# Moving ScalarE's roundings behind copies and squares, and the modulation steps to other places, in a two-layer decoder trunk

## The chip, the cores and the metric

The kernel runs on one core of a Trainium2 chip. The metric is the device time of one execution in microseconds (us). Three runs of the kernel before took 1254.53, 1255.86 and 1257.47 us, with a median of 1255.86 us. The profile shows one further execution.

## The reference

The reference is a decoder trunk of two layers over 512 tokens of 1024 channels, in float32. Layer 0 mixes tokens with a state-space model (S5), layer 1 with forgetting attention (FoX, 16 heads of 64). Behind each mixer stands a gated network with a causal convolution of width 3. Each of the four sub-layers is normalised, shifted, scaled and gated by numbers made from a conditioning vector `c` ("modulation").

```
def modulate(x, g, shift, scale):
    return rmsnorm(x, g) * (1.0 + scale) + shift
...
    mod = jax.nn.silu(c) @ w + b                      # per sub-layer: 3 x 1024 outputs
    shift, scale, gate = jnp.split(mod, 3, axis=-1)
...
    log_f = jax.nn.log_sigmoid((f_logit + b_f).astype(f32))     # fox
    F = lax.cumsum(log_f, axis=1).transpose(0, 2, 1)
    s = q k^T + F[..., None] - F[:, :, None, :]        # causal softmax, then @ v, then @ w_out
...
    up = h @ w_up                                     # network, D_FF = 2816
    a, b = jnp.split(up, 2, axis=-1)
    a_conv = causal width-3 convolution of a
    return (jax.nn.silu(a_conv) * b) @ w_down
```

## The kernel before, in words

All activations lie channel by token, in eight tiles of 128 channels by 512 tokens. Each float32 product is made from two rounded parts per operand: `put_parts` writes `hi`, the rounding of a tile, on ScalarE (ACT, line 256), and `lo`, the rest, on VectorE (DVE, line 257), and TensorE (PE) adds the products hi*hi, lo*hi and hi*lo (line 273). A weight tile comes from memory as `raw` and becomes `w_hi` and `w_lo`; there are five buffers of each of the latter two.

**The program's stages in time.** S5 and its products run to 285 us, with the first network's opening products from about 205 us on in between; the first network runs to 605 us, its last product, the norm, the attention's values and the forget logits to 690 us, the attention's heads to 860 us, the attention's output product and norm to 935 us, the second network to 1200 us, and its tail to 1252 us.

**The networks** (`ffn`) loop over 22 columns f of 128 gated channels. In most columns `quarters` makes both halves of the up-product with seven half-size products of 256 tokens (`times`, line 523) in place of eight, by a Strassen scheme. For that DVE makes four weight sums (`sums`, line 495) of the two `raw` tiles, and ACT and DVE round those as well. The products accumulate in PSUM tiles `p1`, `p5` (`mmp`) and `p2`, `p4` (`aux`). `p1` is used in steps: once a11*b11 is in it, ACT copies it to `nm_h` (line 530, `c1`), s2*t2 is added and it is copied again (`c2`), then s3*t3 is added. So PE can't add s3*t3 before ACT has made the copy `c2`. `gated` then makes the convolution (ACT line 570, two DVE steps at line 572), the activation (ACT line 575), the gating product (DVE line 579) and its rounding (`ghi`, `glo`). Columns 0, 1, 2, 3, 6, 11 and 17 of the first network are made plainly, without sums. Behind each column stand one or two tiles of the down-product (`down`) of the group of columns before.

**The modulation steps** (`ada_units`) are background work: a weight tile of 512 KB is brought by a DMA that GpSimd (POOL) issues at line 213 into a room (`ada_raw` in the first network), and one DVE instruction (line 226) multiplies and sums it. A call of `tick(n)` issues n such steps where it stands, and `behind(...)` orders a step behind the instructions in `self.evac`. In the first network a tick stands ahead of and behind each column's down-product, and `evac` names the last rounding `glo`. In the attention the rooms are the tiles `s3`, `phi` and `plo`, and later weight buffers that `w_hi` and `w_lo` share.

**The squares.** The norm's sum of squares is gathered while the last product still runs: after each residual step (DVE `h`, line 339) ACT squares the tile (`nm_t`, line 331), DVE adds it to `ssq` (line 333), and PE sums over the channels (`aux<-ones,ssq`, line 357). ACT also rounds the attention's first weights (`fox_vf`, `fox_v`) in this stretch.

**The forget logits.** The values' product (line 1317) also gives 16 logits a token. `log_forget` is a chain of 37 small DVE steps on 128x64 elements (`lf_ring`, up to `lf_out` at line 693). PE waits for it at line 1277 (the running sum).

A scheduler places each instruction in its engine's queue by readiness and the edges that the code adds; each engine then works its queue in order.

Of the kernel before, what the change touches and what calls it, by code (L numbers as in the profile page):

```python
# [17 lines left out]
P = 128  # L18
# [30 lines left out]
THIRDS = ((1, 2), (2, 0), (2, 1), (2, 2), (3, 0), (3, 1), (3, 2))  # L49
QK = 6  # L50
# [7 lines left out]
class Trunk:  # L58
# [6 lines left out]
    def __init__(self, tc, io, ctx):  # L65
# [14 lines left out]
        self.normed, self.evac = [], []  # L80
# [116 lines left out]
    def ada_units(self, *thirds, rooms=("ada_raw",), late=True):  # L197
# [3 lines left out]
        todo = [(i, t, j) for i, t in thirds for j in range(KT)]  # L201
# [17 lines left out]
        for n, (i, t, j) in enumerate(todo):  # L219
            if not late:  # L220
                load(n + ahead)
            if j == 0:
                sums = self.bgpool.tile([P, KT], F32, name="ada_s", bufs=2)
# [99 lines left out]
    def square(self, m, cols, eng=None):  # L323
# [7 lines left out]
        nc.scalar.activation(sq[:, cols], self.h[:, m, cols], AF.Square)  # L331
# [155 lines left out]
    def quarters(self, pool, l, f, x, finish):  # L487
# [8 lines left out]
        w = {}  # L496

        def parts(src, names, *where):
# [3 lines left out]
            self.put_parts(hi, lo, src)  # L502
# [25 lines left out]
        def copy(o):  # L528
            t = self.tmp.tile([P, N], F32, name="nm_h", bufs=4)
            nc.scalar.activation(t, o, AF.Copy)  # L530
            return t
# [11 lines left out]
        c2 = copy(p1)  # L543
# [10 lines left out]
    def ffn(self, i, l, x, nxt, ticks=0, plain=None):  # L554

        nc, tc = self.nc, self.tc
        with tc.tile_pool(name=f"ffn{l}", bufs=1, reuse_waits="tile") as pool:
# [8 lines left out]
            def gated(m, ps, cols):  # L566
                f = m // 2
                if m % 2 == 0:
                    t = pool.tile([P, S], F32, name="conv", bufs=2 if plain else 3)
                    nc.scalar.activation(t, ps, AF.Identity, bias=cb[:, f:f + 1], scale=cw[:, 2, f:f + 1])  # L570
                    for d in (1, 2):
                        nc.vector.scalar_tensor_tensor(
# [3 lines left out]
                    keep[f] = t  # L576
                    return
# [8 lines left out]
                self.evac = [self.put_parts(hi[:, j, :], lo[:, j, :], t).ins]  # L586
# [12 lines left out]
            for q, n in enumerate(groups):  # L599
# [6 lines left out]
                for j, f in enumerate(fs):  # L606
# [14 lines left out]
                    if q:  # L621
                        self.tick(ticks)
# [125 lines left out]
class S5(Trunk):  # L748
# [292 lines left out]
    def s5(self, i, nxt):  # L1041
# [186 lines left out]
        with tc.tile_pool(name="s5b", bufs=1, reuse_waits="tile") as pool:  # L1228
# [10 lines left out]
            self.bg = [self.ada_units((1, 2), rooms=("ada_raw", "ada_raw2"))]  # L1239
# [11 lines left out]
class Kernel(S5):  # L1251
# [32 lines left out]
    def fox_values(self, pool, x):  # L1284
# [9 lines left out]
        def load(q):  # L1294

            src = self.io["fox_v"][q - 1] if q else self.io["fox_vf"]
            n, step = (W, 4) if q else (W + NH, 3)
            out = []
            for a in range(0, KT, step):
                j = min(step, KT - a)  # L1300
                hi, lo = self.split(src[:, a:a + j, :], [P, j, n])
                out += [(hi[:, i, :], lo[:, i, :]) for i in range(j)]
            return out

        def values(qs, blocks, w, aux=()):
# [15 lines left out]
            for q, b in todo:  # L1321
# [3 lines left out]
                if b % 2:  # L1325
                    self.tick(1)
# [3 lines left out]
        w = {q: load(q) for q in range(2)}  # L1330
# [4 lines left out]
        for q in range(2, NV):  # L1335
            values((q,), range(NB), {q: load(q)})
        return lf

    def fox(self, i, x, nxt):
        with self.tc.tile_pool(name="fox", bufs=1, reuse_waits="tile") as pool:  # L1340
            self.bgpool = pool
            self.fox_heads(pool, x)
            after, y = nxt
            self.product(
                self.io["fox_w_out"], range(KT), KT, lambda k: (self.o[k][:, 0], self.o[k][:, 1]),
                self.add_residual(i), head=4, tail=2, after=after,
                halves=(slice(0, S),), step=self.unit, ticks=1,
# [3 lines left out]
    def fox_heads(self, pool, x):  # L1351
# [14 lines left out]
        def project(m, ps, cols):  # L1366
# [11 lines left out]
            self.evac = [part.ins]  # L1378
            if m % 2 == 0:
# [205 lines left out]
```

## Time and profile before

| | |
|---|---|
| median of 3 runs | 1255.86 us (1254.53 to 1257.47) |
| profiled execution | 1253.84 us, of which the span of the profile is 1252.0 us |
| PE busy | 1214.2 us, 97% |
| DVE busy | 1007.0 us, 80% |
| ACT busy | 612.4 us, 49% |
| GpSimd busy | 89.1 us, 7% |
| first network, 205 to 605 us | PE 392.02 us, DVE 342.11 us, ACT 186.31 us |
| second network, 935 to 1200 us | PE 265.00 us, DVE 224.63 us, ACT 142.15 us |

A row of the waits reads: engine and line that waited, the engine and line that ended the wait, the sum in us, how often, the longest. A row of the timeline reads: start, duration, engine, line, operation, what it writes and from what, with the idle time ahead of it in brackets. PEclk is the share of its full clock that the throttle granted TensorE.

### The profile page before, as it was taken

To read this page: it belongs to the slowest core of one execution; us is meant where nothing else is said; L and a number is where in the kernel's file an instruction comes from. 1 tells how busy PE (TensorE), PEld (TensorE's weight loads), DVE (VectorE), ACT (ScalarE), POOL (GpSimd) and SP (SyncE) were. 2 spreads that over 40 slices of the span, in tenths; PEclk is the share of its full clock that TensorE was granted. 3 is DMA by queue.
4 is the path that set the end of the run, shared out by engine and by line. 5 is a ranking of instruction groups with operands and counts; after the bars stand their busy time and mean duration, and the time that the engine had idled before them with its cause. 6 is when DMAs were issued, how large, how long until landed. Compare 5 with 4: busy or idle time off the path is not lost.

```text
span 1252.0 us, 20635 instructions
## 1 busy us (share of the span) xinstructions
PE 1214.2 (97%) x7921; PEld 1038.0 (83%) x7921; DVE 1007.0 (80%) x1871; ACT 612.4 (49%) x1137; POOL 89.1 (7%) x143
## 2 busy tenths in 40 slices
PE   7999999999999989999998999999999999999997
PEld 2566678898989889899798888877989999999987
DVE  7888986779889988888777577865799888888855
ACT  3544465335544444444533465663356545555543
POOL 0000000100000000000000344530000000000000
PEclk9999999999999989999999999999999999999999
DMA  9677778521354545443615544422213332332321
GB/s 366 227 231 241 220 226 280 194 80 43 126 183 137 184 153 173 147 160 131 213 52 188 170 145 147 166 82 68 87 51 110 118 120 83 106 119 89 102 85 68
DMA packets 74385, 183.83 MB, mean 147 GB/s; under 512 B 23231, under 2 KB 25631, under 8 KB 73263
## 3 DMA queue, kind: packets, MB, share of 16 engines
q1 hardware_dynamic: 68239, 161.02, 38.5%
q0 software_dynamic: 5760, 20.97, 5.0%
q8 instruction: 62, 1.02, 0.3%
q10 hardware_dynamic: 288, 0.52, 0.1%
q14 instruction: 36, 0.29, 0.1%
HBM read 175.57 MB, written 6.92 MB: 146 GB/s over the span
## 4 chain that ended last, share of the span: by engine, by line
PE 66%; issue 19%; DVE 8%; DMA 4%; ACT 1%; POOL 1%; SPq 0%; DVEq 0%; POOLq 0%; ACTq 0%
PE mmp L273 28%; PE mmp L523 12%; PE aux L523 5%; PE mmp L1131 4%; DVE w_lo L257 2%; PE aux L937 2%; PE mmp L1317 2%; PE aux L1468 2%; PE mmp L1160 2%; PE aux L1026 1%; PE mmp L184 1%; PE aux L1018 1%; PE aux L1451 1%; PE aux L1421 1%; DMA raw<-in_w_up 1%
## 5 line engine op out<-in xcount | busy, mean ns | idle before, releaser
L256 ACT ACTIVATE w_hi<-raw 128x1024 fp32r<-128x1024 f32 (+4 forms) x205 | 176.7, 866 | 168.4 <-PE mmp L273 81.3
L257 DVE TENSOR_TENSOR w_lo<-raw,w_hi 128x1024 fp32r<-128x1024 f32 (+4 forms) x205 | 202.0, 992 | 30.3 <-ACT w_hi L256 30.0
L273 PE MATMUL mmp<-ghi,w_hi 128*128 128x512 f32 (+1 forms) x392 | 148.2, 378 | 0.0
L273 PE MATMUL mmp<-glo,w_hi 128*128 128x512 f32 (+1 forms) x392 | 147.6, 376 | 0.0
L273 PE MATMUL mmp<-ghi,w_lo 128*128 128x512 f32 (+1 forms) x392 | 147.3, 376 | 0.0
L273 PE MATMUL mmp<-a_hi,w_hi 128*128 128x512 f32 (+1 forms) x376 | 139.5, 374 | 1.5 <-ACT a_hi L410 1.5
L273 PE MATMUL mmp<-a_lo,w_hi 128*128 128x512 f32 (+1 forms) x376 | 137.2, 365 | 0.0
L273 PE MATMUL mmp<-a_hi,w_lo 128*128 128x512 f32 (+1 forms) x376 | 137.1, 365 | 0.0
L523 PE MATMUL mmp<-w_hi 128*128 128x256 f32 x396 | 111.8, 282 | 7.0 <-ACT nm_h L530 7.0
L523 PE MATMUL mmp<-w_lo,w_hi 128*128 128x256 f32 x396 | 110.9, 280 | 0.0
L523 PE MATMUL mmp<-w_hi,w_lo 128*128 128x256 f32 x396 | 110.7, 279 | 0.0
L256 ACT ACTIVATE w_hi<-sums 128x1024 fp32r<-128x1024 f32 x74 | 78.4, 1059 | 56.6 <-DVE sums L495 43.2
L257 DVE TENSOR_TENSOR w_lo<-sums,w_hi 128x1024 fp32r<-128x1024 f32 x74 | 90.3, 1220 | 5.0 <-ACT w_hi L256 4.5
L339 DVE SCALAR_TENSOR_TENSOR h<-mmp,par,h 128x512 f32<-128x512 f32 (+1 forms) x100 | 68.4, 684 | 25.8 <-PE mmp L273 25.5
L273 PEld LDWEIGHTS mmp<-ghi,w_lo 128*128 128x128 f32 x392 | 75.2, 192 | 14.4
L273 PEld LDWEIGHTS mmp<-ghi,w_hi 128*128 128x128 f32 x392 | 75.5, 193 | 13.0
L273 PEld LDWEIGHTS mmp<-glo,w_hi 128*128 128x128 f32 x392 | 75.3, 192 | 12.9
L273 PEld LDWEIGHTS mmp<-a_hi,w_hi 128*128 128x128 f32 x376 | 70.9, 190 | 14.4 <-issue 2.6
L523 PEld LDWEIGHTS mmp<-w_hi 128*128 128x128 f32 x396 | 75.6, 191 | 8.0 <-ACT nm_h L530 8.0
L273 PEld LDWEIGHTS mmp<-a_hi,w_lo 128*128 128x128 f32 x376 | 71.4, 190 | 12.0 <-DVE w_lo L257 0.6
L273 PEld LDWEIGHTS mmp<-a_lo,w_hi 128*128 128x128 f32 x376 | 71.4, 190 | 9.9
L523 PEld LDWEIGHTS mmp<-w_lo,w_hi 128*128 128x128 f32 x396 | 75.2, 190 | 0.0
(313 smaller groups left out, 3013.5 us busy)
## 6 DMA issues: line engine op xcount, KB each, us to landing
raw<-in_w_up SPq DMA_DIRECT2D x88, 512.0 KB, 3.3
raw<-in_ada_w SPq DMA_DIRECT2D x40, 512.0 KB, 6.4
ada_raw<-in_ada_t POOLq DMA_DIRECT2D x40, 512.0 KB, 3.9
raw<-in_w_down SPq DMA_DIRECT2D x32, 320.0 KB, 3.2
nf<-nfd SPq DMA_DIRECT2D x8, 1152.0 KB, 6.4
raw<-in_fox_qk SPq DMA_DIRECT2D x16, 512.0 KB, 4.4
raw<-in_w_down SPq DMA_DIRECT2D x24, 256.0 KB, 3.3
raw<-in_w_down SPq DMA_DIRECT2D x16, 384.0 KB, 3.1
```

Of the source, the lines that this page charges most:

```text
L184: self.last_mm = nc.tensor.matmul(ps[32 * qq:32 * qq + 32, :], self.sc32[:, k, :], w[:, q * S:(q + 1) * S], start=(step is steps[0]), stop ...
L256: nc.scalar.activation(hi, src, AF.Copy)
L257: return nc.vector.tensor_tensor(lo, src, hi.bitcast(F32), ALU.subtract)
L273: self.last_mm = self.nc.tensor.matmul(o, wt, xt[:, cols], start=(k == 0 and n == 0), stop=(k == nk - 1 and n == 2),)
L339: add = self.nc.vector.scalar_tensor_tensor(self.h[:, m, cols], ps, self.par[i][:, 16 + m:17 + m], self.h[:, m, cols], op0=ALU.mult, op1=A ...
L523: self.last_mm = nc.tensor.matmul(o, wt[:, k], xt[:, k], start=(first and k == 0 and n == 0), stop=(k == H - 1 and n == 2), skip_group_che ...
L937: nc.tensor.matmul(ps[g2][:, j, cols], x[rows, a + j, r].rearrange("p c j -> p (c j)"), self.rr[rows, planes, q, :], start=(j == 0 and r = ...
L1018: nc.tensor.matmul(yp[g2][:, k, :], t[:, g].rearrange("p c i -> p (c i)"), u[:, g, :], start=(k == 0), stop=False, skip_group_check=True,)
L1131: nc.tensor.matmul(ps, w[m][:, k, :], x[:, k], start=(k == 0), stop=(k == KT - 1))
L1160: nc.tensor.matmul(gps[m], wt, xt[:, k], start=(k == 0 and part == 0 and xt is yhi), stop=(k == KT - 1 and part == 1))
L1317: self.last_mm = nc.tensor.matmul(ps[q, b][:, :n], xt[:, k, tb], wt, start=(k == 0 and i == 0), stop=(k == KT - 1 and i == 2),)
L1468: nc.tensor.matmul(pv[:, c * P:], self.v[:, hp, k, r].rearrange("p t d -> p (t d)"), pp[:, r, c + 3 * k:NB + 3 * k, :].rearrange("p b t -> ...
```

## The change

No instruction is added or taken away: the change is one of order, with the rooms of some modulation steps.

- In `quarters`, the roundings of a column stand behind the copy `c2` of the column before (`self.copied`).
- In the first network, the first of a column's two ticks moves from behind the column to the end of the convolution's second DVE step, and the steps are ordered behind that step instead of behind `glo`.
- The roundings of the attention's first weights, but the first piece of each, stand behind the last square of the first half (`self.squared`), and the pieces of two quarters of heads alternate.
- Among the attention's values, ticks stand at five blocks of the first two quarters of heads (before: at every second block of all), so that steps stand ahead of the forget chain and not inside it.
- In the heads, the tick moves from the projections to behind the last rounding of a head pair's turned weights (`plo`).
- The last two steps are given the rooms `s3` and `nf` in place of weight buffers, and ticks at tiles 4 and 5 of the output product.

The diff, cut:

```diff
@@ squares
+            a = nc.scalar.activation(sq[:, cols], self.h[:, m, cols], AF.Square)
+        if m == KT - 1 and cols.start == 0:
+            self.squared = [a.ins]
@@ quarters
+        copied = self.copied
...
-            self.put_parts(hi, lo, src)
+            with self.behind(*copied):
+                self.put_parts(hi, lo, src)
...
-        def copy(o):
+        def copy(o, last=False):
             t = self.tmp.tile([P, N], F32, name="nm_h", bufs=4)
-            nc.scalar.activation(t, o, AF.Copy)
+            a = nc.scalar.activation(t, o, AF.Copy)
+            if last:
+                self.copied = [a.ins]
             return t
...
-        c2 = copy(p1)
+        c2 = copy(p1, True)
@@ gated, in ffn
-                        nc.vector.scalar_tensor_tensor(
+                        c = nc.vector.scalar_tensor_tensor(
                             t[:, d:], ps[:, :S - d], cw[:, 2 - d, f:f + 1], t[:, d:], op0=ALU.mult, op1=ALU.add
                         )
                     nc.scalar.activation(t, t, AF.Silu)
                     keep[f] = t
+                    if plain and f >= groups[0]:
+                        self.evac = [c.ins]
+                        self.tick(ticks)
                     return
...
-                self.evac = [self.put_parts(hi[:, j, :], lo[:, j, :], t).ins]
+                self.put_parts(hi[:, j, :], lo[:, j, :], t)
@@ ffn
                     if q:
-                        self.tick(ticks)
                         down(q - 1, range(j * KT // n, (j + 1) * KT // n))
                         self.tick(ticks)
@@ fox_values
+        def load(qs):
+
+            out = {q: [] for q in qs}
+            for c in range(3):
+                for q in qs:
...
+                    with self.behind(*(self.squared if 0 in qs and c else ())):
+                        hi, lo = self.split(src[:, a:a + j, :], [P, j, n])
...
-                if b % 2:
+                if todo[0][0] == 0 and (b != 1 or q):
                     self.tick(1)
@@ fox
+            def add(m, ps, cols):
+                residual(m, ps, cols)
+                if m in (4, 5):
+                    self.tick(1)
...
-                halves=(slice(0, S),), step=self.unit, ticks=1,
+                halves=(slice(0, S),), step=self.unit,
@@ fox_heads
-            self.evac = [part.ins]
-            if m % 2 == 0:
+            if m == 0:
                 self.tick(1)
@@ turn
+            if b == NB - 1:
+                self.evac = [part.ins]
+                self.tick(1)
@@ the whole
-        k.bg = [k.ada_units((3, 1), rooms=("s3", "phi", "plo"), late=False), k.ada_units((3, 0), rooms=(1, 2), late=False)]
+        k.bg = [
+            k.ada_units(units((3, 1))[:7], rooms=("s3", "phi", "plo"), late=False),
+            k.ada_units(units((3, 1))[7:] + units((3, 0))[:6], rooms=(1, 2), late=False),
+            k.ada_units(units((3, 0))[6:], rooms=("s3", "nf"), late=False),
+        ]
```

**What it moves, at three places.** The first is ACT's queue in column 12 of the first network, at about 444 us of the profile. The numbers behind the names are those of the buffers; `mmp_4305` is column 12's `p1`, while the `raw` and `sums` tiles are those of column 13. Before:

```order
L530 ACTIVATE nm_h_4323<-mmp_4305 128x256
L530 ACTIVATE nm_h_4337<-mmp_4306 128x256
L256 ACTIVATE w_hi_4470<-raw_4464 128x1024
L256 ACTIVATE w_hi_4476<-sums_4468 128x1024
L530 ACTIVATE nm_h_4364<-mmp_4305 128x256
L256 ACTIVATE w_hi_4486<-raw_4466 128x512
```

After the change:

```order
L536 ACTIVATE nm_h_4323<-mmp_4305 128x256
L536 ACTIVATE nm_h_4337<-mmp_4306 128x256
L536 ACTIVATE nm_h_4364<-mmp_4305 128x256
L258 ACTIVATE w_hi_4470<-raw_4464 128x1024
L258 ACTIVATE w_hi_4476<-sums_4468 128x1024
L258 ACTIVATE w_hi_4486<-raw_4466 128x512
```

The copy `c2` (the third `nm_h`) moved ahead of the two roundings.

The second is ACT's queue at the squares, at about 612 us; the `raw` tiles are the first weights of the attention's values. Before:

```order
L256 ACTIVATE w_hi_6396<-raw_6398 128x544
L331 ACTIVATE nm_t_6064<-h_1962 128x512
L256 ACTIVATE w_hi_6402<-raw_6404 128x1024
L331 ACTIVATE nm_t_6090<-h_1962 128x512
L256 ACTIVATE w_hi_6408<-raw_6410 128x1024
L331 ACTIVATE nm_t_6116<-h_1962 128x512
L331 ACTIVATE nm_t_6160<-h_1962 128x256
```

After the change:

```order
L333 ACTIVATE nm_t_6090<-h_1962 128x512
L333 ACTIVATE nm_t_6116<-h_1962 128x512
L333 ACTIVATE nm_t_6160<-h_1962 128x256
L333 ACTIVATE nm_t_6180<-h_1962 128x256
L333 ACTIVATE nm_t_6200<-h_1962 128x256
L333 ACTIVATE nm_t_6220<-h_1962 128x256
L258 ACTIVATE w_hi_6396<-raw_6398 128x816
L258 ACTIVATE w_hi_6402<-raw_6404 128x1024
L258 ACTIVATE w_hi_6408<-raw_6410 128x544
```

Three roundings moved behind seven squares (the first stands ahead of this piece, `nm_t_6064`).

The third is DVE's queue at the head of the output product, at about 861 us; `raw` under line 226 (228 after the change) is the room of a modulation step, and `w_lo_8814` (`w_lo_8809` after) the weight of output tile 4. Before:

```order
L339 SCALAR_TENSOR_TENSOR h_1962<-mmp_8538,par2_97,h_1962 128x512
L226 ISA raw_8434,ada_s_7175<-raw_8434,c_row_1970 128x1024
L226 ISA ada_s_7175 128x1
L339 SCALAR_TENSOR_TENSOR h_1962<-mmp_8539,par2_97,h_1962 128x512
L233 TENSOR_TENSOR par3_98<-ada_s_7175,rest_126 128x8
L339 SCALAR_TENSOR_TENSOR h_1962<-mmp_8540,par2_97,h_1962 128x512
L333 TENSOR_TENSOR ssq_8797<-ssq_8797,nm_t_8802 128x512
L339 SCALAR_TENSOR_TENSOR h_1962<-mmp_8541,par2_97,h_1962 128x512
L333 TENSOR_TENSOR ssq_8797<-ssq_8797,nm_t_8806 128x512
L257 TENSOR_TENSOR w_lo_8814<-raw_8815,w_hi_8813 128x1024
```

After the change, from a place some 32 rows earlier in the queue, while the last head pair still runs:

```order
L228 ISA raw_8284,ada_s_7445<-raw_8284,c_row_1970 128x1024
L228 ISA ada_s_7445 128x1
L259 TENSOR_TENSOR w_lo_8528<-raw_8529,w_hi_8527 128x1024
L259 TENSOR_TENSOR lo_8502<-mmp_8437,hi_8501 128x512
L259 TENSOR_TENSOR w_lo_8809<-raw_8810,w_hi_8808 128x1024
```

The rounding of tile 4's weight moved ahead of the last head pair's work; the last modulation steps now stand behind tile 4's and tile 5's residual steps (not shown).

More of the change, by code (lines that the diff above doesn't have):

```diff
@@ L195, in ada_pe, with ada_units @@
             yield True
-    def ada_units(self, *thirds, rooms=("ada_raw",), late=True):
+    def ada_units(self, todo, rooms=("ada_raw",), late=True):
         nc = self.nc
-        todo = [(i, t, j) for i, t in thirds for j in range(KT)]
         ws = {}
@@ L221, in ada_units @@
                 load(n + ahead)
[L222 to L223 removed]
+            if (i, t) not in self.sums:
+                self.sums[i, t] = self.bgpool.tile([P, KT], F32, name="ada_s", bufs=2)
+            sums = self.sums[i, t]
             w = ws.pop(n)
```

33 lines of the change are left out of this document (17 added, 16 removed).

## The prediction

> **What bounds the kernel now.** I read the page's first part, then the waits of TensorE (PE), then the stretches around each of them, then the timelines of ACT and DVE there. The page says who is busy:
>
> ```profile
> PE 1214.2 (97%) x7921; PEld 1038.0 (83%) x7921; DVE 1007.0 (80%) x1871; ACT 612.4 (49%) x1137; POOL 89.1 (7%) x143
> ```
>
> PE is the bound, and only time in which it waits or runs at a lower clock can be won by a change of order. The waits of PE (who waited, for whom, sum, times, longest) name it:
>
> ```profile
> PE mmp L523 <- ACT nm_h L530: 7.0, 4, 3.2
> ...
> PE mmp L1277 <- DVE lf_out L693: 4.2, 1, 4.2
> PE aux L357 <- DVE ssq L333: 2.9, 1, 2.9
> PE mmp L273 <- DVE w_lo L257: 2.5, 1, 2.5
> ...
> PE mmp L273 <- DVE lo L257: 0.8, 1, 0.8
> ...
> PE aux L1468 <- DVE plo L257: 0.5, 2, 0.4
> ```
>
> These six rows are the places that the change touches: 7.0 + 4.2 + 2.9 + 2.5 + 0.8 + 0.5 = 17.9 us. The waits have a second price, in the stretches behind them (start:end, length, busy time of PE, PEld, DVE, ACT, POOL, granted clock, DMA share, GB/s):
>
> ```profile
> 205.00:605.00 400.00, 392.02 (x2423) 350.70 (x2423) 342.11 (x540) 186.31 (x287) 20.14 (x38) 0.99 0.44 148
> 361.00:420.00 59.00, 57.24 (x412) 53.47 (x411) 51.20 (x82) 27.80 (x46) 4.24 (x8) 1.00 0.48 161
> ...
> 625.00:631.00 6.00, 6.00 (x28) 6.00 (x29) 1.78 (x10) 0.64 (x2) 0.00 (x0) 0.50 0.20 80
> ...
> 860.00:935.00 75.00, 71.29 (x427) 62.72 (x426) 63.20 (x112) 36.72 (x54) 0.00 (x0) 0.98 0.24 79
> 935.00:1200.00 265.00, 265.00 (x1875) 247.38 (x1873) 224.63 (x333) 142.15 (x220) 0.00 (x0) 1.00 0.33 106
> ...
> 448.00:453.80 5.80, 5.80 (x20) 5.12 (x21) 5.52 (x9) 3.12 (x5) 0.00 (x0) 0.50 0.47 147
> 689.00:692.50 3.50, 3.50 (x12) 2.69 (x11) 1.21 (x1) 0.00 (x0) 0.00 (x0) 0.54 0.86 301
> 867.00:870.20 3.20, 3.20 (x8) 2.52 (x9) 2.73 (x3) 0.00 (x0) 0.00 (x0) 0.50 0.61 187
> ```
>
> After the long waits PE runs at about half its clock: 5.80 us at 0.50 lose 2.9 us, 6.00 at 0.50 lose 3.0, 3.50 at 0.54 lose 1.6, 3.20 at 0.50 lose 1.6, together 9.1. So the six rows with their clock are worth 27.0 us, the most that the change can bring.
>
> The Trainium skill, "TensorE: Matmul & The Clock Gate", section "What's actually happening", says that TensorE falls to half its clock after at least one idle window of about 3.4 us, and that the window is free-running. The rows above have half clock behind waits of 2.9 and 2.5 us, so here shorter waits did it too. By that length alone, the clock behind those two would not come back with the waits, and the sum below would be 4.6 us poorer; the rows decide, and I keep it.
>
> **First network: copies ahead of roundings.** ACT's queue at the longest of the four waits, and PE's end of it:
>
> ```profile
> 446.61 1.06 ACT L256 ACTIVATE w_hi<-sums 128x1024 fp32r<-128x1024 f32 x1 [5.08 <-DVE sums L495]
> 447.57 0.37 ACT L530 ACTIVATE nm_h<-mmp 128x256 f32<-128x256 f32 x1
> ...
> 447.99 0.58 PE L523 MATMUL mmp<-w_hi 128*128 128x256 f32 x1 [3.22 <-ACT nm_h L530]
> ```
>
> ACT sat idle for 5.08 us with a rounding of column 13 at its head, whose sums DVE had not made; the copy that PE needed came behind it. With the copy first, ACT's idle time covers it, and all four waits (7.0) and the half clock (2.9) go: 9.9 us. What is queued behind the copy now are the roundings: each waits for the copy of the column before, at a time when before it could have run. That is free while DVE's work, w_lo behind w_hi, arrives before PE wants it. The price lies with DVE, because the modulation steps move as well:
>
> ```profile
> DVE ada_raw L226 <- DMA ada_raw<-in_ada_t: 20.3, 18, 2.4
> DVE sums L495 <- DMA raw<-in_w_up: 12.5, 10, 2.1
> ...
> L226 DVE CUSTOM_DVE_ANT_0 ada_raw<-ada_raw,c_row x40: 1215/1222/1228, 225.8 to 587.7; 128x1024 f32<-128x1024 f32 x40
> L213 POOL DMA_DIRECT2D ada_raw<-in_ada_t x38: 530/530/532, 227.3 to 580.3; - x38
> ```
>
> The two steps of a column now stand further apart, which takes away DVE's waits for the one room that they share (20.3 us, 18 times), but the first step, 1.22 us, stands ahead of the column's own sums and roundings. In columns 7 to 10 DVE is busy 51.20 of 59.00 us, and there is the danger: in columns 9 and 10 the next columns' sums stand behind a step, and the weight tile of column 10 is fetched later, since the buffer that it takes is freed behind that step. Per column this costs nothing if the 7.8 us of DVE idleness there absorb it, and at worst one step and the longest wait of sums for their tile, 1.22 + 2.1 = 3.3 us; for two columns 0 to 6.6. Following the two queues of the changed order by hand, with the durations of the trace, I get stalls of some 1 to 3 us in each, the middle of that; I take 4.0. The other columns with two down tiles keep room. POOL's 530 ns to issue and SP's loads move with the steps and aren't waited for by anything else. Term: -9.9 + 4.0 = -5.9, bounds -9.9 to -3.3.
>
> **The squares.**
>
> ```profile
> 612.38 0.61 ACT L331 ACTIVATE nm_t<-h 128x512 f32<-128x512 f32 x1
> 615.43 1.06 ACT L256 ACTIVATE w_hi<-raw 128x1024 fp32r<-128x1024 f32 x1 [2.44 <-DMA raw<-in_fox_v]
> 616.39 0.61 ACT L331 ACTIVATE nm_t<-h 128x512 f32<-128x512 f32 x1
> ...
> 616.52 1.23 DVE L257 TENSOR_TENSOR w_lo<-raw,w_hi 128x1024 fp32r<-128x1024 f32 x1 [1.97 <-ACT w_hi L256]
> ```
>
> ACT and DVE stand still for 2.44 and 1.97 us with a rounding at their heads whose weight has not landed, and the squares queue behind. With the squares first, L357 comes almost on time: 2.9 of wait and 3.0 of clock, 5.9 us. What is late next: three roundings at up to 1.23 us on DVE (and three w_hi of about 1 us on ACT) now fall into the short DVE steps of the norm, between L357 and the start of the values' product. Between nothing hidden (3.7 lost) and all hidden lies the truth; the norm's steps leave DVE idle much of that time, but the roundings run in one piece each. I take 2.4 lost, nearer the far end. Term: -3.5, bounds -5.9 to -2.2.
>
> **The forget logits.**
>
> ```profile
> 672.26 0.79 DVE L257 TENSOR_TENSOR v<-mmp,v 128x256 fp32r<-128x256 f32 x2 [5.37 <-ACT v L256]
> ...
> 674.44 0.22 DVE L693 SCALAR_TENSOR_TENSOR lf_ring<-ft 128x64 f32<-128x64 f32 x1
> ...
> 685.01 1.22 DVE L226 CUSTOM_DVE_ANT_0 s<-s,c_row 128x1024 f32<-128x1024 f32 x1
> ...
> 688.36 0.22 DVE L693 SCALAR_TENSOR_TENSOR lf_out<-lf_ring 128x64 f32<-128x64 f32 x1
> ```
>
> The chain runs 674.44 to 688.58 = 14.1 us; it starts only after DVE has idled 5.37 us for the values of the next heads, and contains two modulation steps of 1.22. After the change it stands ahead of those values, with one step inside: it can start up to 5 us earlier and is 1.2 shorter. PE arrives 4.2 us too early before, so the chain ends about when PE comes. What is late next: a rounding and the evacuation of PSUM behind the chain, for which I leave 0.7. Term: -(4.2 + 1.6) + 0.7 = -5.1, bounds -5.8 to -3.0 (the step and half of the idle time won only, and the clock lost again).
>
> **The heads.** The rows "L273 <- lo" and "L1468 <- plo" stand where a modulation step lies ahead of the last roundings of a pair. The step moves behind them; the next column's roundings follow it. Term: -1.3, bounds -1.3 to 0.5 worse, if one step of 1.22 comes to lie ahead of another awaited rounding.
>
> **The output product's head.**
>
> ```profile
> 860.22 2.01 ACT L256 ACTIVATE w_hi<-raw 128x1024 fp32r<-128x1024 f32 x2 [1.32 <-PE mmp L273]
> ...
> 861.12 1.22 DVE L226 CUSTOM_DVE_ANT_0 raw<-raw,c_row 128x1024 f32<-128x1024 f32 x1
> ...
> 865.64 1.22 DVE L257 TENSOR_TENSOR w_lo<-raw,w_hi 128x1024 fp32r<-128x1024 f32 x1
> 866.91 0.80 PE L273 MATMUL mmp<-v,w_lo 128*128 128x512 f32 x1 [2.55 <-DVE w_lo L257]
> ```
>
> The weight of tile 4 gets its buffers late, as modulation steps hold two of them, and its rounding ends at 866.86. With other rooms for the last steps it is rounded during the last head pair. Tile 5's comes just in time. The two moved steps (2.4 us of DVE, and their two loads on SP) lie in the output product and its norm, where DVE is busy 63.20 of 75.00 us. Term: -(2.5 + 1.6) = -4.1, bounds -4.1 to -1.5.
>
> **The second network** gets the same edge for its 18 columns made by quarters, and no steps. PE never waits there (265.00 of 265.00); DVE is busy 224.63, so about 40 us, 2.2 a column, are free. A rounding held back by a copy has about that much room. I cost it at nothing; the cover is that room.
>
> **The sum.** -5.9 - 3.5 - 5.1 - 1.3 - 4.1 = -19.9 us, against the profiled execution of 1253.84 us (span 1252.0 and 1.8 around it): 1233.9. The median of the three runs, 1255.86, lies 2.0 above the profiled execution; so I expect a median of 1236 us.
>
> **Rivals.** *All is kept:* the roundings that I charge are hidden everywhere; -27.0 gives 1229. For it: DVE idles 20% of the span; against it: the first network's DVE is busy 342 of 400. *DVE takes the first network's part back:* stalls of 3 us with half clock behind them in columns 9, 10 and some of 18 to 20 eat the 9.9; -14.0 is left (the other four terms), 1242; with the squares' gain gone too, 1245. The Trainium skill, "Perfetto Trace Analysis", section "Identifying the Most-Contended Engine", warns that PE's busy share is no good measure of its limit; by its advice PE's weight loads, 350.70 of 400 us, would be set against DVE's 342.11, which makes the two near equals here. *Slower: the edge makes the second network late.* There w_lo, now released by a copy, comes after PE wants it, in each of 18 columns. From 19.9 / 18 = 1.1 us a column on the whole gain is gone; at one long rounding and its w_lo, 1.06 + 1.22 = 2.3 us, it costs 41 us and the time is 1277. For it: such a column loses no time now, so anything can only be worse; against it: the 2.2 us of room, and that the copies come in the first half of a column, the roundings being wanted in the next. *No change:* the scheduler places the roundings where they stood. The queues of the changed program show the copies first, so this is all but excluded; it could only come about by gains and losses that cancel.
>
> **Chances.** The forecast, near -20 (1231 to 1240): 0.48. All kept: 0.12. First network's gain taken back or more, still faster: 0.22. Cancelled within 0.2% (2.5 us, about what a measurement can tell): 0.06. Slower, by the second network or by many stalls with half clock in the first: 0.12. So faster 0.82, same 0.06, slower 0.12. The range reaches from just under all kept, 1228, to the two squandered parts and some more, 1250; it leaves out what is slower or the same.
>
> **What would show it.** In the changed profile the row "mmp L523 <- ACT nm_h" should be gone, no clock of 0.5 at 447 to 454, 625 to 631 and 867 to 870, DVE's wait for ada_raw below 10 us, lf_out within a microsecond of PE. It is wrong if PE waits at L523 for w_lo or w_hi, in columns 8 to 10 or in the second network, for more than 10 us in all, or if L1317 starts no earlier, beside L357, than before.

## The result, and the profile after

The changed kernel took 1249.11 us (median of 16 runs, 1246.01 to 1255.90), the kernel before 1255.91 (16 runs beside them); the ratio is 0.994, with a 95% interval of 0.9919 to 0.9962. It is faster by some 7 us, a third of the 20 that I had summed up. The profiled execution has a span of 1249.2 us, against 1252.0.

The waits of PE in the first network (361 to 622 us) of the changed kernel:

```profile
PE mmp L529 <- DVE w_lo L259: 3.6, 2, 2.8
PE mmp L529 <- ACT w_hi L258: 2.1, 2, 1.2
PE aux L529 <- DVE w_lo L259: 1.9, 1, 1.9
PE mmp L529 <- ACT nm_h L536: 0.6, 2, 0.3
```

The 7.0 us for nm_h are down to 0.6, as forecast. In their place stand 7.6 us for weights that are rounded too late, which before were not waited for. The stretches that answer to those of before (start:end, length, busy time of PE, PEld, DVE, ACT, POOL, granted clock, DMA share, GB/s):

```profile
361.00:420.00 59.00, 53.62 (x354) 49.58 (x352) 50.05 (x80) 24.95 (x41) 4.22 (x8) 0.94 0.41 141
...
625.00:631.00 6.00, 6.00 (x52) 6.00 (x52) 2.97 (x7) 1.85 (x5) 0.00 (x0) 1.00 0.00 0
689.00:692.00 3.00, 3.00 (x15) 2.47 (x14) 1.54 (x2) 0.00 (x0) 0.00 (x0) 1.00 0.36 123
867.00:870.00 3.00, 3.00 (x14) 2.42 (x13) 3.00 (x5) 0.30 (x1) 0.00 (x0) 1.00 0.53 175
935.00:1200.00 265.00, 265.00 (x1887) 247.86 (x1886) 221.21 (x331) 139.87 (x221) 0.00 (x0) 1.00 0.32 106
...
389.00:420.00 31.00, 25.62 (x155) 23.37 (x153) 25.50 (x42) 11.72 (x20) 2.11 (x4) 0.89 0.37 128
```

The last of these stretches in the kernel before:

```profile
389.00:420.00 31.00, 30.82 (x216) 28.52 (x215) 26.92 (x43) 15.76 (x27) 2.12 (x4) 1.00 0.52 176
```

Behind the squares, the logits and the output product's head the clock is full where it was half. In columns 7 to 10 PE is busy 53.62 us where it was 57.24, and the clock has a new dip (0.89 from 389 to 420 us, 1.00 before).

To see where the time went, I compared two traces at points where PE has the same work behind it (the matmuls started so far, each counted with its usual length, since their order differs a little from kernel to kernel). From these points follows how much longer (+) or shorter (-) each part is than in the kernel before, in us. "Network" is 361 to 622 us of before, "squares" 622 to 644, "logits" 644 to 700, "heads" 700 to 860, "head" (the output product's) 860 to 878, "rest" 878 to 1200. The first row is the sum that I had put down; the others are worked out from the traces named.

| | network | squares | logits | heads | head | rest | sum |
|---|---|---|---|---|---|---|---|
| predicted | -5.9 | -3.5 | -5.1 | -1.3 | -4.1 | 0 | -19.9 |
| changed | +4.4 | -5.3 | -5.5 | +5.0 | -5.0 | 0.0 | -6.3 |
| net_ticks_back | +0.5 | -5.3 | -5.7 | +4.8 | -5.0 | 0.0 | -10.7 |
| copies_free | +8.7 | -5.3 | -5.7 | +5.3 | -5.0 | +0.2 | -1.7 |
| heads_back | +4.7 | -5.3 | -5.7 | +0.4 | -5.0 | 0.0 | -10.8 |
| both_back | +2.9 | -5.0 | -5.3 | +0.2 | -5.0 | 0.0 | -12.1 |
| hold_back | +3.5 | -5.2 | -5.7 | +0.1 | -5.0 | +1.2 | -11.1 |
| hold_ot | +4.2 | -5.2 | -5.7 | +10.1 | -5.0 | 0.0 | -1.6 |
| two_only | +10.0 | -5.0 | -5.7 | +0.1 | -5.0 | 0.0 | -5.6 |
| raw4_wb4 | -10.8 | -5.7 | -5.3 | -0.6 | -3.2 | +4.1 | -21.5 |
| before_raw4 | -1.3 | -5.7 | -4.8 | +3.4 | -5.0 | +2.7 | -10.7 |
| both_back_raw4 | -6.7 | -5.6 | -5.0 | -0.5 | -3.2 | +2.2 | -18.8 |
| raw4_lo5 | -10.8 | -5.7 | -4.4 | -0.5 | -3.2 | +3.8 | -20.8 |
| raw4_hi5 | -10.6 | -5.6 | -3.7 | +1.0 | -3.4 | +5.3 | -17.2 |

So four terms were about right and two had the wrong sign: the first network, 10.3 us off, and the heads, 6.3 us off.

How the stall in column 9 came about, in the changed kernel's trace (SP's loads, DVE, PE, in order of time; in column 8 two modulation steps lie 5.5 us apart):

```profile
376.40 10.03 SPq L167 DMA_DIRECT2D raw<-in_w_up  x2
...
378.74 1.22 DVE L228 CUSTOM_DVE_ANT_0 ada_raw<-ada_raw,c_row 128x1024 f32<-128x1024 f32 x1
...
384.21 1.22 DVE L228 CUSTOM_DVE_ANT_0 ada_raw<-ada_raw,c_row 128x1024 f32<-128x1024 f32 x1
...
385.35 1.29 DVE L259 TENSOR_TENSOR w_lo<-raw,w_hi 128x512 fp32r<-128x512 f32 x2
...
390.88 0.69 DVE L499 TENSOR_TENSOR sums<-raw 128x512 f32<-128x512 f32 x1 [3.90 <-DMA raw<-in_w_up]
...
399.90 0.58 PE L529 MATMUL mmp<-w_hi,w_lo 128*128 128x256 f32 x1 [2.81 <-DVE w_lo L259]
```

The row of SP holds the two loads of a column's weights, and ends with the second: it is issued 10 us behind the first, at 386.1, since it needs one of three raw buffers, and DVE's rounding that frees one (385.35) stands behind a modulation step. DVE starts on the tile at 390.88, 4.8 us behind the issue, after idling 3.90 us for it, and nine us later PE waits 2.81 us for what is made from it. In the kernel before the second load of this pair is issued 2 us behind the first:

```profile
371.89 2.40 SPq L165 DMA_DIRECT2D raw<-in_w_up  x2
```

In the heads, DVE's queue in the changed kernel:

```profile
733.88 1.81 DVE L228 CUSTOM_DVE_ANT_0 raw<-raw,c_row 128x1024 f32<-128x1024 f32 x1
...
735.62 2.30 DVE L259 TENSOR_TENSOR w_lo<-raw,w_hi 128x1024 fp32r<-128x1024 f32 x1
737.84 0.68 DVE L259 TENSOR_TENSOR lo<-mmp,hi 128x512 fp32r<-128x512 f32 x1
738.44 1.21 DVE L259 TENSOR_TENSOR w_lo<-raw,w_hi 128x1024 fp32r<-128x1024 f32 x1
739.57 1.39 DVE L1498 TENSOR_TENSOR ot<-ot,aux 64x512 f32<-64x512 f32 x2
```

```profile
740.30 0.44 PE L1441 MATMUL aux<-hi 64*128 64x384 f32 x1 [0.23 <-DVE ot L1498]
741.02 0.44 PE L1441 MATMUL aux<-hi 64*128 64x384 f32 x1 [0.28 <-DVE ot L1498]
```

The step and two long roundings now stand ahead of `ot`, which empties the PSUM tile of the attention's output. PE's next logits need that tile, and from 690 to 860 us its waits have a row that the kernel before has not (2.2 us; heads_back below tests what the place costs in all):

```profile
PE aux L1441 <- DVE ot L1498: 2.2, 8, 0.4
```

In the kernel before DVE sat idle ahead of `ot`, waiting for ACT:

```profile
739.17 0.68 DVE L1475 TENSOR_TENSOR ot<-ot,aux 64x512 f32<-64x512 f32 x1 [1.75 <-ACT ot L1474]
```

### The profile page after: what moved, and what is told of

It reads as the page before. It is cut to its first block, busy times and chain, and to the rows that moved or that the text cites. A ratio compares the mean times of both kernels' runs of the same rounds, so it can differ in the third digit from the quotient of the medians.

```text
span 1249.2 us, 20558 instructions
## 1 busy us (share of the span) xinstructions
PE 1217.2 (97%) x7921; PEld 1039.6 (83%) x7921; DVE 1010.6 (81%) x1871; ACT 609.2 (49%) x1137; POOL 83.3 (7%) x143
## 4 chain that ended last, share of the span: by engine, by line
PE 70%; issue 14%; DVE 8%; DMA 5%; ACT 1%; POOL 1%; SPq 0%; DVEq 0%; POOLq 0%; ACTq 0%
PE mmp L275 29%; PE mmp L529 14%; PE aux L529 6%; PE mmp L1141 4%; PE mmp L1332 2%; DVE w_lo L259 2%; PE aux L947 2%; DMA raw<-in_w_up 2%; PE mmp L1170 2%; PE aux L1036 1%; PE aux L1471 1%; PE mmp L186 1%; PE aux L1028 1%; DVE ada_raw L228 1%; PE mmp L1081 1%
## 5 line engine op out<-in xcount | busy, mean ns | idle before, releaser
L258 ACT ACTIVATE w_hi<-raw 128x1024 fp32r<-128x1024 f32 (+5 forms) x205 | 175.9, 865 | 145.5 <-PE mmp L275 61.2
L259 DVE TENSOR_TENSOR w_lo<-raw,w_hi 128x1024 fp32r<-128x1024 f32 (+5 forms) x205 | 207.0, 1017 | 49.1 <-ACT w_hi L258 48.8
L536 ACT ACTIVATE nm_h<-mmp 128x256 f32<-128x256 f32 x99 | 37.5, 381 | 111.3 <-PE mmp L529 111.0
```

The lines of the kernel that those rows point to most:

```text
L258: nc.scalar.activation(hi, src, AF.Copy)
L259: return nc.vector.tensor_tensor(lo, src, hi.bitcast(F32), ALU.subtract)
L536: a = nc.scalar.activation(t, o, AF.Copy)
```

## The experiments

All kernels are edits of the changed one unless said otherwise; ratios are against the kernel before on the same chip, with 95% intervals.

**net_ticks_back.** The first network's steps go back to where they stood.

```diff
-                    if plain and f >= groups[0]:
-                        self.evac = [c.ins]
-                        self.tick(ticks)
...
+                self.evac = [self.put_parts(hi[:, j, :], lo[:, j, :], t).ins]
...
                     if q:
+                        self.tick(ticks)
                         down(q - 1, range(j * KT // n, (j + 1) * KT // n))
```

> The changed kernel with the modulation steps of the first network back where they were (ahead of and behind each column's down-product, ordered behind glo); the copies ahead of the roundings, and all else of the change, stay. In the changed kernel's trace the first network (361 to 605 us of before) lost 4.3 us instead of gaining 9.9. Theory 'steps': the step of 1.22 us behind the convolution holds back DVE's sums and roundings in columns 9, 10 and 15, so with the steps back the stalls at L529 for w_lo and w_hi (7.6 us, with half clock behind two of them) go, and the four waits for nm_h stay away: 9 to 14 us less than the changed kernel, about 1236 to 1240. Rival 'edge': the roundings, held behind the copies, are late by themselves; then the stalls in columns 9 and 10 stay and the time is within 3 us of the changed kernel's 1249.

Measured: 1248.09 us, ratio 0.9906 (0.9873 to 0.9940). The network is 3.9 us shorter than in the changed kernel, not 9 to 14: the stalls of columns 9 and 15 are gone, but waits for nm_h are back (here 5.5, in both_back 6.0), at other columns. In both_back the longest stands so (ACT's queue and PE):

```profile
478.58 0.74 ACT L258 ACTIVATE w_hi<-raw 128x640 fp32r<-128x640 f32 x1 [1.22 <-DMA raw<-in_w_down]
479.22 0.64 ACT L536 ACTIVATE nm_h<-mmp 128x256 f32<-128x256 f32 x2
```

```profile
479.64 0.39 PE L529 MATMUL mmp<-w_hi 128*128 128x256 f32 x1 [2.38 <-ACT nm_h L536]
```

The rounding at the head of ACT's queue is now that of a down weight which has not landed; the edge does not cover it. So both theories miss a part: the step does the harm in columns 9 and 15, and the edge does not remove the waits for nm_h once the order is another. By the ratios the whole is some 4 us shorter than in the changed kernel.

**copies_free.** Steps moved, no edge on the roundings.

```diff
-            with self.behind(*copied):
+            with self.behind():
                 self.put_parts(hi, lo, src)
```

> The changed kernel without the edge that puts the roundings of a column behind the copy c2 of the column before, in both networks; the moved steps stay. Theory 'steps': the stalls for w_lo and w_hi in columns 9 and 10 stay, and waits for nm_h come back beside them (up to 7.0 us, and a clock drop of 2.9): 2 to 10 us slower than the changed kernel. Rival 'edge': the stalls for w_lo and w_hi go, waits for nm_h of up to 7 come back, about the changed kernel's time or 4 us less. The second network should not change (under 1 us) by either.

Measured: 1259.43 us, ratio 0.9987 (0.9962 to 1.0013). The waits for w_lo and w_hi in columns 9, 10 and 15 stay and those for nm_h come back (4.4 us, 2 times, longest 3.1); the network is 4.3 us longer than in the changed kernel, and the second network, from 935 to 1200 us, the same within 0.1. That is the theory of the steps. With net_ticks_back and the kernel before it makes a table of four, as the network's length against before: neither 0, edge alone +0.5 (in both_back +2.9), steps alone +8.7, both +4.4. Neither half of the change gains anything in the network by itself while there are three raw buffers.

**heads_back.** The heads' steps go back to the projections.

```diff
-            if m == 0:
+            self.evac = [part.ins]
+            if m % 2 == 0:
                 self.tick(1)
...
-            if b == NB - 1:
-                self.evac = [part.ins]
+            if b == NB - 1 and hp == KT - 1:
                 self.tick(1)
```

> The changed kernel with the heads' modulation steps back at the projections' evacuations (every second one). Theory: in the changed kernel the step, 1.8 us there, and a long rounding stand ahead of ot, the evacuation of the attention's output, so the PSUM tile that PE wants next comes free late (L1441 waits for ot, 8 times), which cost about 5 us from 690 to 862; back in place, that wait goes and the waits of before (plo, lo: 1.3) return: 3 to 5 us less than the changed kernel. Rival: the five us come from GpSimd's or DMA's work at other times and not from the step's place; then the L1441 waits stay and the time is within 1.5 us of the changed kernel.

Measured: 1246.09 us, ratio 0.9896 (0.9866 to 0.9927). The heads are 4.6 us shorter, and no row for ot is left. As expected; the gain that I had looked for is not there either, for what plo and lo cost before is now a wait of 1.5 for lo in one place:

```profile
PE mmp L275 <- DVE lo L259: 1.5, 1, 1.5
PE aux L1442 <- DVE mn L1454: 0.6, 1, 0.6
PE aux L1491 <- DVE plo L259: 0.3, 2, 0.2
```

**both_back.** net_ticks_back and heads_back together.

> Both undone together: steps of the first network and of the heads back in their old places, with the copies, the squares, the forget logits and the output product's head as changed. If the two losses are separate, the two gains add: 12 to 18 us less than the changed kernel, about 1232 to 1237; by the theory 'edge' only the heads' part, about 1245.

Measured: 1244.90 us, ratio 0.9876 (0.9840 to 0.9912). The plain time is that of the theory 'edge'; by the ratios the kernel is some 8 us shorter than the changed one, between the two expectations. The network gives back 1.5 of its 4.4 us here and 3.9 in net_ticks_back, though both kernels have the same order of instructions in it: so far can two profiles of one order lie apart in this part, and smaller differences between single profiles show nothing.

**hold_back.** both_back, and the roundings of the other weights of the first network (the function `split`) stand behind the copy too.

```diff
-        self.put_parts(hi, lo, self.raw(shape, src))
+        raw = self.raw(shape, src)
+        with self.behind(*(self.copied if self.hold else ())):
+            self.put_parts(hi, lo, raw)
```

> Steps of the first network and of the heads in their old places (as in both_back), and in the first network the roundings of the down-product's weights and of the plain columns' weights stand behind the last copy c2 as well. In both_back and net_ticks_back PE still waits 5.5 to 6.0 us, 4 times, for a copy nm_h: now a rounding of a down weight that DMA has not brought, or of a plain column's weight, stands ahead of the copy. Theory 'the head of ACT's queue': the edge only moved the wait to the next rounding without an edge; with the edge on those too the row for nm_h falls under 1 us, and 361 to 622 us of before is 4 to 6 us shorter than in both_back, if DVE then still makes w_lo of the down weights in time. Rival 'DVE': the roundings now come too late, new waits for w_lo at L275 take what is won, and the time stays within 2 us of both_back.

Measured: 1243.59 us, ratio 0.9891 (0.9863 to 0.9919). No wait for nm_h is left, and DVE's roundings come late instead:

```profile
PE mmp L532 <- DVE w_lo L262: 8.0, 11, 1.6
PE mmp L532 <- ACT w_hi L261: 1.5, 2, 0.8
```

The network is 0.6 us longer than in both_back, which is less than two profiles of one order differ by. The rival holds in its sum, though the late weights are those of the up-product and not of the down-product: with this order, too, something is late by as much.

**hold_ot.** hold_back with the heads' step behind the attention output's last rounding.

```diff
-            self.put_parts(o[:, 0], o[:, 1], ot)
+            self.evac = [self.put_parts(o[:, 0], o[:, 1], ot).ins]
+            if hp < KT - 1:
+                self.tick(1)
```

> hold_back, but the heads' modulation step stands behind the attention output's evacuation of each pair (ot and its rounding) in place of the projections' evacuation. Theory: the step harms where it lies ahead of something whose PSUM or rounding PE wants; behind ot, only the next pair's logits (s from aux, wanted by ACT and the turn) follow, so the wait at L275 for lo (1.3 to 1.5) goes and none for ot comes: 0 to 2 us less than hold_back. Rival: the step delays the next pair's masked logits instead, 1 to 3 us more.

Measured: 1257.18 us, ratio 0.9974 (0.9949 to 0.9998). My theory was wrong and the rival right by more than it said: the heads are 10.0 us longer. The step now stands ahead of the masked logits and delays them, and by them GpSimd's scaling and PE's transposes; 5.2 of the 10.0 us stand in this row:

```profile
PE aux L1474 <- POOL s L1465: 5.2, 11, 1.0
```

**two_only.** heads_back, with the first network's step behind the convolution only in columns with two down tiles.

```diff
-                    if plain and f >= groups[0]:
+                    if plain and f >= groups[0] and self.two:
...
                     if q:
+                        if not self.two:
+                            self.tick(ticks)
```

> heads_back, with the first network's first step moved behind the convolution only in columns with two down tiles, and left ahead of the down-product in columns with one. By my prediction the harm of the moved step is in the columns 8 to 10, where one down tile leaves PE the shortest column and DVE no room. Theory: then the stalls in columns 9 and 10 (9.4 us from 389 to 420 of before in the changed kernel) mostly go, and the waits of about 6 us for nm_h that came back with the steps in their old places stay away in the columns with two: 361 to 622 us of before is 6 to 9 us shorter than in heads_back. Rival: column 9 has two down tiles, so the step stays in it, and the stall with it: within 2 us of heads_back.

Measured: 1249.97 us, ratio 0.9939 (0.9914 to 0.9964). The network is 5.3 us longer than in heads_back, worse than either expectation; the stalls of columns 9 and 10 stay (5.6 and 3.5 us from 389 to 420), and others come up near 480 us. What PE waits for is again late weights:

```profile
PE mmp L529 <- DVE w_lo L259: 7.6, 9, 1.8
PE mmp L529 <- ACT w_hi L258: 2.9, 3, 1.2
```

**raw4_wb4.** The changed kernel with four raw buffers, and four of `w_hi` and of `w_lo` each.

```diff
-RAW, WB = 3, 5
+RAW, WB = 4, 4
```

> The changed kernel with four buffers for raw weight tiles (before three) and four for w_hi and w_lo each (before five; five of each with four raw ones do not fit). Theory 'late load': the stall in column 9 begins with a weight tile whose DMA is issued only when the raw buffer that it takes is freed by a rounding behind the moved step; with a fourth raw buffer DVE's wait of 3.9 us for that tile at 391 us and the stall behind it shrink to under 1 us. What four buffers of w_hi and w_lo cost is not known and may show as waits elsewhere. Rival 'DVE's work': the sums are late because DVE is full; the wait for the DMA goes but PE's wait for w_lo stays at 2 us and over.

Measured: 1238.16 us, ratio 0.9830 (0.9807 to 0.9853). It loses 3.6 us between 285 and 361 us, ahead of the table's parts, in a wait of 2.3 for w_lo. But in the whole stretch from 361 to 620 us PE waits for nothing that makes a row, and the network is 10.8 us shorter than before: the whole of what I had put down gross (9.9) came. The cause shows in ACT's and DVE's waits for a loaded tile from 361 to 620 us; of the changed kernel:

```profile
ACT w_hi L258 <- DMA raw<-in_w_up: 25.6, 14, 3.9
...
DVE sums L499 <- DMA raw<-in_w_up: 11.3, 5, 3.9
```

and of raw4_wb4:

```profile
ACT w_hi L258 <- DMA raw<-in_w_up: 4.3, 3, 3.0
...
DVE sums L499 <- DMA raw<-in_w_up: 3.1, 3, 2.3
```

and of the kernel before:

```profile
ACT w_hi L256 <- DMA raw<-in_w_up: 16.4, 7, 4.2
...
DVE sums L495 <- DMA raw<-in_w_up: 2.1, 3, 0.9
```

So the change made late loads worse, and these made the stalls. With three raw buffers DVE's row is 8.7 to 13.9 us in the four kernels with a moved step in the network (changed, copies_free, heads_back, two_only) and 2.1 to 3.9 in those without (before, net_ticks_back, both_back, hold_back, hold_ot), while ACT's row is 23.0 to 32.3 in all of them but before: it is DVE's row that goes with the step. DVE's load of work is the same in both kernels, 1010.6 and 1007.9 us; the rival, that DVE is simply full, falls. That it is the fourth raw buffer and not the fewer buffers of `w_hi` and `w_lo` is shown by raw4_lo5 and raw4_hi5 below, which have five of the one or the other and the same network, -10.8 and -10.6. The heads' loss is gone too, with the step in its new place: in most pairs one rounding of a weight now stands between the step and `ot`, where the changed kernel has two.

**before_raw4.** The kernel before with the same edit.

> The kernel before (nothing of the change) with four raw buffers and four of w_hi and w_lo each. raw4_wb4, the changed kernel with these numbers, took 1238.2 us against 1249.1 of the changed kernel, and its first network (361 to 602 us of before) was 10.8 us shorter than that of before. Theory 'late load under the new order': raw tiles bound only the changed order, since it keeps them longer; then here the four waits for nm_h (7.0) stay and the network is within 3 us of before, the time within 4 us of before. Rival 'buffers alone': the fourth raw tile does the work by itself; then the nm_h waits fall under 2 us here too and the time is some 6 to 10 us below before.

Measured: 1249.00 us, ratio 0.9912 (0.9886 to 0.9939). In the network the theory holds: it is 1.3 us shorter only, and the waits for nm_h stay:

```profile
PE mmp L523 <- ACT nm_h L530: 5.4, 4, 1.9
```

For the whole it misses, as I had asked only about the network: squares, logits and the output product's head are 5.7, 4.8 and 5.0 us shorter without any of the change. At the squares the stall had come from a rounding at the head of a queue whose tile had not landed, so either the order or the load can be mended; what the buffers do to the other two was not followed up. It gives back 3.4 us in the heads and 2.7 behind 878 us, there with waits of 0.5 and 2.7 for w_lo.

**both_back_raw4.** both_back with the same edit.

> both_back (edge on the copies, squares, logits and head as changed; the steps of first network and heads in their old places) with four raw buffers and four of w_hi and w_lo each. If the moved step in the network is good once loads are early, this is slower than raw4_wb4, by the waits for nm_h of some 3 to 6 us that came back in both_back; if the step's place does not matter, both have the same network part within 1.5 us. In the heads raw4_wb4 has no wait for ot, though the step stands in its new place; so 690 to 860 should be equal within 1 us.

Measured: 1242.10 us, ratio 0.9859 (0.9830 to 0.9888), slower than raw4_wb4 by 4.1 us in the network, with a wait of 2.0 for nm_h and what follows it. So, by one profile of this kernel, the moved step is good in the network once loads are early, and harmful while they are late: with four raw buffers the network against before is -1.3 with neither part of the change, -6.7 with the edge and -10.8 with both (the steps without the edge were not run). The heads are equal within 0.1, as expected.

**raw4_lo5 and raw4_hi5.** raw4_wb4 with a fifth buffer of `w_lo`, and of `w_hi`.

> The changed kernel with four raw buffers, four of w_hi and five of w_lo (as many in all as before). raw4_wb4 still waits for w_lo at L275 near 310 us, 2.3, with half clock, 3.6 together, and loses 4.7 us between 871 and 935 us; if that is for want of w_lo buffers it goes here, and the time is 4 to 8 us below raw4_wb4's 1238; if it is for want of w_hi buffers, nothing changes and raw4_hi5 has the gain.

> The same with five buffers of w_hi and four of w_lo. The other side of raw4_lo5: a gain of 4 to 8 us here if w_hi's buffers are what lacks (ACT's rounding runs ahead of DVE's and holds its tile longer, which speaks for this one), else nothing.

Measured: 1238.07 us, ratio 0.9822 (0.9795 to 0.9849), and 1245.71, ratio 0.9885 (0.9858 to 0.9912). Neither brings the gain. The fifth `w_lo` changes nothing beside raw4_wb4; with the fifth `w_hi` the wait near 310 us takes another form (1.9 and 2.2 us for w_lo, at two products), and the stretch from 285 to 361 us is 6.6 us longer than before, not 3.6. What makes w_lo late there and behind 871 us stays open; in raw4_wb4 PE waits at the same product of both networks, 2.28 us at 310 and 2.56 at 914, so the place belongs to the opening of a network. raw4_lo5 and raw4_wb4 are the fastest kernels here, some 21 us below the kernel before on the same chip.

## Why the prediction was right and wrong

The direction was right, and the measured median lies in the range, at its upper end; the sum was three times too large. None of the signs of being wrong that I had named came: PE waits 7.6 us for late weights in the first network, under the 10 that I had set, so that sign was too coarse.

*First network: wrong, -5.9 put down, +4.4 measured.* The gross gain of 9.9 was read well: at the old stalls 1.8, 5.5 and 1.9 us came back, and 10.8 in all with another raw buffer. The failing step is the price of the moved modulation step, 4.0 between bounds of 0 and 6.6. Its mechanism was the right one, down to the columns (the tile of the next column is fetched later, as its buffer comes free behind the step), but it cost 9.4 us in columns 9 and 10 and 4.3 in column 15, together 13.7. Three things were missing in it: the upper bound added one step to one late tile and left out that late tiles hold up their followers; the half clock behind a new stall of 2.81 us, though the rows of before showed it for waits as short; and column 15, which I had called roomy. The rival that DVE takes the first network's part back was near what came, with chance 0.22; its name was wrong, since what lacked was a raw buffer and not DVE's time. That the median still lies in the range is in part luck: the two terms with the wrong sign, 16.6 us off together, just fit into its width.

*Squares: -5.3 for -3.5,* inside its bounds, at the good end: the three roundings fell among the norm's short DVE steps (632 to 637 us of the changed kernel), and PE waits 0.3 us in all from 620 to 700. *Logits: -5.5 for -5.1.* The chain starts at 668.3 (674.4 before) with one step inside it, as forecast, and lasts 13.1 us; PE no longer waits at that line. (The code sets the ticks at seven blocks of the values, not at five as the list of the change says.) *Head: -5.0 for -4.1,* a little past its best bound. These three terms came true in all kernels with three raw buffers. *Second network:* nothing, as put down (0.0 from 935 to 1200).

*Heads: wrong, -1.3 put down, +5.0 measured.* The bound of 0.5 worse counted one step of 1.22 us ahead of one awaited rounding. It lay ahead of `ot` in each pair, in most with two roundings (2.30 and 1.21 us) behind it, and took 1.8 us itself; heads_back shows that its place cost 4.6. I had named the next column's roundings as what follows the step and not asked who waits behind those.

*Clock.* "TensorE: Matmul & The Clock Gate" of the Trainium skill, section "What's actually happening", puts the fall to half clock at one idle window of about 3.4 us. Here the clocks behind the waits of 2.9 and 2.5 us came back with them, and so did that behind the wait of 3.22 us, which is shorter than 3.4 as well and which I had left out of that comparison (by that length alone the sum would be 7.5 us poorer, not 4.6). The new wait of 2.81 us, with one of 0.94 ahead of it, brought a dip (0.89 from 389 to 420), and in column 15 two waits of 1.18 and 0.76 us were enough:

```profile
497.00:501.00 4.00, 2.07 (x16) 1.66 (x14) 4.00 (x7) 1.96 (x3) 0.00 (x0) 1.00 0.38 131
501.00:505.00 4.00, 4.00 (x21) 4.00 (x22) 2.89 (x5) 1.93 (x3) 0.53 (x1) 0.57 0.21 47
```

A single wait of 2.03 us at 519 us of the kernel before was not followed by a dip (1.00 from 519 to 524). So in these traces the length of one wait does not tell whether the clock falls, and two short ones close together can do it.

## What to carry to other kernels

An engine that works in order stalls on the first instruction whose operand is missing, so a row "PE waits for a copy by ACT" can be a load that came late: look at what ACT and DVE waited for just ahead, and count the buffers of the tile that was not there. Ordering edges then only choose who is late next; in the first network the new order gave its full gain of 10 us only with a fourth raw buffer, and cost 4 without. A background step that is moved is priced by all that queues behind it until the next wait of the bottleneck engine, not by its own length.

## What the runs showed of the hardware

The start of the program, which the change doesn't touch, differed from run to run. From 20 to 200 us the granted clock and the length changed between profiles:

```profile
20.00:200.00 180.00, 177.52 (x1327) 115.30 (x1324) 150.35 (x258) 83.99 (x227) 1.29 (x2) 0.99 0.75 246
```

is the kernel before, and of copies_free:

```profile
20.00:200.00 180.00, 177.50 (x1284) 113.26 (x1283) 145.04 (x248) 80.57 (x221) 1.28 (x2) 0.93 0.71 231
```

At 200 us the same matmul started 3.4 us later in the changed kernel's profile than in that of before, 9.4 later in copies_free's and 0.2 in hold_back's. A few us in the total of one profile are therefore no evidence, and I compared kernels by parts of the trace.

In the heads of the changed kernel a DVE rounding of 128x1024 took 2.30 us and a modulation step 1.81, beside this work of GpSimd; where GpSimd did nothing, each took 1.22:

```profile
733.31 3.53 POOL L1419 TENSOR_TENSOR nf<-nf,rest 128x512 f32<-128x512 f32 x2 [3.79 <-DMA nf<-nfd]
```

The same rounding at 738.44, behind GpSimd's two, took 1.21. From 690 to 870 us the six such roundings that begin beside GpSimd's work on `nf` took 2.29 to 2.32 us, the twelve beside no work of GpSimd 1.21 to 1.23. In hold_ot, where the seven steps of the heads stand beside no work of GpSimd, each took 1.22. The roundings `lo`, with one operand in PSUM, took 0.68 or 0.69 us beside GpSimd as elsewhere. No run took GpSimd's work away, but the step changed its length with its place. "GPSIMD Engine Reference" of the Trainium skill, "Specifications", says that GpSimd's interfaces to SBUF are shared with VectorE, with contention for DVE instructions that have two SBUF inputs. Both slow instructions have two, and the durations agree.
